# A hybrid decoder layer on one core: the third stage's loads on ScalarE, a chunk's queries in token halves, the second block's scores inside its product, the norm row a step earlier, accumulator banks kept

## The chip, the cores and the metric

One core of a Trainium2 chip runs the whole kernel. Its engines are TensorE (PE, with its weight loads shown as PEld), VectorE (DVE), ScalarE (ACT), GpSimd (POOL) and SyncE (SP), which only issues transfers. Transfers are issued by SP, ACT or POOL, in the order of the issuing engine's instructions, and run on 16 DMA engines that all share. The metric is the device time of one execution in microseconds (us); lower is better.

## What is computed

One layer of a hybrid decoder on a prompt of 4096 tokens and on 64 sample tokens (8 sequences of 8), all float32, model width 1024. Three groups of heads work on one projection:

```python
h = _rmsnorm(x, g_pre)
z = h @ w_in                                   # 1024 -> 2816
cb, cc, ch, cg, q, k, v, ag, mq, mg = _split_cols(z)
out_a = jax.nn.silu(cg) * cb * conv            # conv of width 3 over cc * ch
o_b = _window_prompt(q, k, v, sink_g)          # window of 128, 8 query heads, 2 kv heads, sinks
out_b = jax.nn.silu(ag) * o_b
o_c = _mem_attend(mq.reshape(n, t, MEM_HEADS, HEAD_DIM), mem_k, mem_v)   # 256 memory tokens
out_c = jax.nn.silu(mg) * o_c
y = jnp.concatenate([out_a, out_b, out_c], axis=-1) @ w_out
return x + _rmsnorm(y, g_post), new_conv, new_k, new_v
```

The sample tokens attend to cached keys and values of their own. New keys, values and conv states are outputs too.

## The kernel before

Matrices are multiplied at close to float32 precision by splitting each operand into a rounded high part (a copy by ACT) and the rest (a subtraction by DVE), and adding up three products: high x high, high x low, low x high.

**The input projection** (L927 on) runs in three stages over the 22 column tiles of `w_in`. Each stage goes over 8 token blocks of 2 x 260, and each block takes 7 products instead of 8 by sums of operands (`PRODUCTS`, L40). A step is one such product: for every column tile of the stage's pairs 12 matmuls of 128x260 into an accumulator bank, which DVE (or ACT for the first product) adds into `z` (`evict`). A step `i` also splits the operand of step i + 1 (`h_split`: ACT's copy, L364, and DVE's subtraction, L365) and, in the third stage, loads the operand of step i + 3 (`h_load`, L525) into one of four buffers. A load has to wait until the split of the operand that had the buffer is done. In the first stage the order of all engines is written out; from the second stage on a planner orders the instructions by its own costs and by when operands should be ready, except where the code asks for program order. The accumulators are two double banks for even and two for odd steps (`accumulator`, L148). At the start of the third stage all of these are closed and other pools opened: two small banks `psm` for the attention's first groups and the memory's keys, and a double and a single bank for each of the two kinds of step.

The third stage has three column pairs, so a step is 36 matmuls. In its gaps run the memory's keys (`mem_product`), and, from `third_jobs` (L808) at steps counted by n = 7 (b - 1) + p, the scores, softmax, transposes, masks and values of the first attention groups: `EARLY` gives the n of every piece of groups 0, 1 and 2, `PIECES` the pieces. The last block of the stage splits the output weights (`wo_split`, `wo_load`) into slots of the pool `wa`, as the input weights leave them.

**Attention and output** run over 33 blocks: 31 of 128 tokens, the block of the sample tokens, and the last one of 128. `Block.run` (L1516) multiplies the block's mixed heads with `w_out` in two halves of 512 columns, k = 0 to 7, three matmuls each: 48 matmuls of 128x512. Between them it runs events at given (half, k), from `events_of` (L1598). The event `values_and_scores(i)` at the block's beginning (in block 0 at k = 3) takes the scores of group i + 3, in four banks for the window and two for the memory, and the values of group i + 1 in the double bank `pv`. The softmax of a group is done by DVE and ACT, its weights are transposed by DVE in 32x32 squares, and 16 transfers of 64 KB (L1234) put the squares in place: on POOL's queue for groups 0 to 2, on SP's after that. POOL masks them (`masks`, L1248), and the values are due at the start of a later block. Each half of a block's product is scaled by the norm row `gpost` into `yn` (DVE, L1544) and squared (ACT, L1545); only then is its bank free. Queries and keys come in chunks of 256 tokens, two groups each (`chunk_load`, L1336), on POOL's queue, the queries in two transfers, one for the high and one for the low parts. The norm row is loaded at L1591, behind the projection. DVE and PE keep program order through these blocks, ACT in block 0 and POOL in blocks 1 and 2.

The sample tokens' attention is spread over blocks 26 to 30 by a table (L1594): `sample_window` (L1409) loads its mask into `smraw` (L1423) in its first part, makes scores and softmax in its second, transposes in its third (`swt`) and multiplies in its fourth.

Names: `x_6T` is a third-stage operand of block 6, `hi_` and `lo_` its parts, `c` an accumulator, `s` a group's scores and weights, `w` the weights in place, `wd` a masked copy, `ws` and `xs` window and memory scores, `pv` the values, `y` an output product, `mh` and `ml` the parts of the mixed heads.

Of the kernel before, what the change touches and what calls it, by code (L numbers as in the profile page):

```python
# [8 lines left out]
F32 = mybir.dt.float32  # L9
# [6 lines left out]
P = 128  # L16
# [35 lines left out]
def hybrid_layer(ctx: ExitStack, tc: tile.TileContext, a: dict):  # L52
# [65 lines left out]
    def open_phase(ph):  # L118
# [16 lines left out]
        if ph != 1:  # L135

            psa.close()
            bank = lambda name, bufs: psa.enter_context(tc.tile_pool(name=name, bufs=bufs, space=bass.MemoryType.PSUM))
            if ph == 0:
                pa2 = bank("pa0", 2)  # L140
            else:

                third["ps"] = bank("psm", 2)
                pa1 = {(tag, w): bank(f"p{tag}{w}", 1) for tag, w in (("y", 2), ("x", 2), ("x", 1), ("y", 1))}

    tp = natp = pa2 = pa1 = None

    def accumulator(i, w, name):  # L148
# [371 lines left out]
    def h_load(i):  # L520
        if i < len(steps) and steps[i][0] == 2:
# [3 lines left out]
            DMA.dma_start(t, hd[b][o])  # L525
# [315 lines left out]
    EARLY = ((15, 16, 17, 18, 19, 22, 24), (22, 23, 24, 25, 26, 29, 31), (30, 31, 32, 33, 34, 37))  # L841
    PIECES = (*(lambda g, n=n: g.early_scores(n) for n in range(4)), lambda g: g.early_turn(), lambda g: g.masks(), lambda g: g.values())
# [72 lines left out]

    last = NBLK - 1
# [10 lines left out]
    def input_projection():  # L927
        for i, (ph, b, p) in enumerate(steps):
# [78 lines left out]
    def open_attention():  # L1007
# [6 lines left out]
        ps = {tag: ctx.enter_context(tc.tile_pool(name=f"ps{tag}", bufs=1, space=bass.MemoryType.PSUM)) for tag in ("pv", *range(6))}  # L1014
# [45 lines left out]
    class Chunk:  # L1060
# [20 lines left out]
        def load_queries(self):  # L1081

            self.q = self.pool(True).tile([P, 12, CT], F32R, tag="q", name=f"q{self.c}").rearrange("p (j a) n -> p j a n", a=2)
            for part in range(2):
                G.dma_start(self.q[:, :, part, :], qd[part, 1:7, :, self.ts].rearrange("j p n -> p j n"))
# [28 lines left out]
    class Group:  # L1114
# [28 lines left out]
        def scores(self):  # L1143
            self.open_scores()
            bands = [psum(n, f"ws{self.b}_{n}").rearrange("p (h k) -> p h k", h=2) for n in range(4)]
            cross = [psum(4 + hh, f"xs{self.b}_{hh}").rearrange("p (j k) -> p j k", j=2) for hh in range(2)]
# [3 lines left out]
            tail(1)  # L1150
            self.crosses(cross)
# [85 lines left out]

        def early_turn(self):
            self.turn_band()
            self.turn_cross()  # L1240
# [511 lines left out]
```

## Time and profile before

| | us |
|---|---|
| median of 3 runs | 1502.98 |
| range of the runs | 1501.84 to 1504.06 |
| the profiled execution | 1499.29 |
| its span, first to last instruction | 1497.6 |

Input projection: the third stage begins at about 668 us and ends at 950 us; attention and output take the rest. The page gives, for each engine, the time in which it was busy as a share of the span, the share of the span in forty slices, the DMA queues, and the chain of work that ended last. A wait line reads: the engine and what it was about to do, then what ended the wait. Line L66 is the helper that keeps program order; there the names of the tiles tell the operation. "issue" is a wait that nothing in the profile explains. Where a wait is put down to something that had long been done, it was for another thing, often a transfer.

### The profile page before, as it was taken

To read this page: it belongs to the slowest core of one execution; us is meant where nothing else is said; L and a number is where in the kernel's file an instruction comes from. 1 tells how busy PE (TensorE), PEld (TensorE's weight loads), DVE (VectorE), ACT (ScalarE), POOL (GpSimd) and SP (SyncE) were. 2 spreads that over 40 slices of the span, in tenths; PEclk is the share of its full clock that TensorE was granted. 3 is DMA by queue.
4 is the path that set the end of the run, shared out by engine and by line. 5 is a ranking of instruction groups with operands and counts; after the bars stand their busy time and mean duration, and the time that the engine had idled before them with its cause. 6 is when DMAs were issued, how large, how long until landed. Compare 5 with 4: busy or idle time off the path is not lost.

```text
span 1497.6 us, 30845 instructions
## 1 busy us (share of the span) xinstructions
PE 1467.0 (98%) x11459; PEld 1341.6 (90%) x11459; DVE 1207.6 (81%) x1890; ACT 757.6 (51%) x1869; POOL 448.4 (30%) x623
## 2 busy tenths in 40 slices
PE   9999999999999999999999998899999999999998
PEld 9999999999999999999999988777777787777766
DVE  6779888898988777797678776878898898989843
ACT  6776666465422222254535443556555666656632
POOL 0223232212300000000003322265566566556531
PEclk9999999999999999999999999999999999999999
DMA  9989999887864333478967978899989988898663
GB/s 264 188 239 224 291 287 275 245 270 257 230 207 166 116 123 111 136 266 278 301 217 219 287 234 298 268 223 248 221 237 233 245 222 224 211 252 218 189 193 100
DMA packets 211964, 337.27 MB, mean 225 GB/s; under 512 B 55269, under 2 KB 125797, under 8 KB 211781
## 3 DMA queue, kind: packets, MB, share of 16 engines
q1 hardware_dynamic: 166629, 253.99, 56.7%
q0 software_dynamic: 43888, 78.15, 21.3%
q10 hardware_dynamic: 1296, 3.15, 0.7%
q8 instruction: 91, 1.49, 0.4%
q14 instruction: 60, 0.49, 0.1%
HBM read 192.48 MB, written 110.15 MB: 202 GB/s over the span
## 4 chain that ended last, share of the span: by engine, by line
PE 78%; DMA 7%; DVE 6%; issue 4%; POOL 2%; SPq 2%; ACT 1%; ACTq 0%; DVEq 0%; POOLq 0%
PE c L374 48%; PE y L66 19%; PE pv L66 5%; PE ws L66 2%; DMA w<-s 1%; PE y L1537 1%; PE xs L66 1%; PE mem_acc L789 1%; DMA x_7T<-hd_T 1%; SPq L1234 1%; DMA gpost<-in_gpost 1%; DVE s L66 1%; DMA vd<-v 1%; DMA wr_2A<-in_w_in 0%; DMA smraw<-in_smask 0%
## 5 line engine op out<-in xcount | busy, mean ns | idle before, releaser
L66 PE MATMUL y<-wo,mh 128*128 128x512 f32 x992 | 318.7, 396 | 0.0
L381 DVE TENSOR_TENSOR z<-c,z 128x520 f32<-128x520 f32 (+1 forms) x308 | 194.4, 644 | 81.6 <-PE c L374 78.2
L66 PEld LDWEIGHTS y<-wo,mh 128*128 128x128 f32 x992 | 186.5, 188 | 52.7 <-DVE wnm L66 5.0
L66 PE MATMUL y<-wo,ml 128*128 128x512 f32 x496 | 193.6, 390 | 0.0
L1193 ACT ACTIVATE s<-s,wnm 128x128 f32<-128x128 f32 x248 | 96.0, 388 | 45.7 <-DVE wnm L66 39.8
L1217 POOL TENSOR_SCALAR s<-s,xrd 128x256 f32<-128x256 f32 x120 | 57.7, 494 | 183.3 <-DVE xrd L66 106.1
L66 PEld LDWEIGHTS y<-wo,ml 128*128 128x128 f32 x496 | 93.5, 188 | 18.2
L1178 ACT COPY s<-ws 128x256 f32<-128x256 f32 x124 | 39.9, 379 | 92.4 <-PE ws L66 72.8
L748 POOL MEMSET negs<- 128x1 f32 x1 | 0.1, 98 | 266.6 <-PE c L374 266.6
L1567 POOL TENSOR_TENSOR xr<-yn,xr 128x1024 f32<-128x1024 f32 x29 | 69.6, 2398 | 21.5 <-ACT yn L1566 21.2
L66 DVE STREAM_TRANSPOSE s<-s 128x1024 f32<-128x1024 f32 x58 | 70.9, 1236 | 5.1 <-POOL s L1217 2.7
L1248 POOL TENSOR_SCALAR_AFFINE_SELECT wd<-w 128x512 f32<-128x512 f32 (+1 forms) x60 | 55.6, 926 | 49.5 <-DMA w<-s 28.8
L66 DVE TENSOR_TENSOR yn<-y,gpost 128x512 f32<-128x512 f32 x62 | 42.3, 683 | 29.5 <-PE y L66 22.7
L1545 ACT ACTIVATE y<-y 128x512 f32<-128x512 f32 (+1 forms) x64 | 37.4, 584 | 51.2 <-DVE yn L66 44.3
L66 PEld LDWEIGHTS ws<-kst,q 64*128 64x128 f32 x696 | 44.3, 189 | 17.2 <-issue 14.2
L1209 ACT ACTIVATE s<-xs,xnm 128x256 f32<-128x256 f32 x124 | 56.3, 461 | 4.4 <-DVE xnm L1207 3.7
L66 PE MATMUL ws<-kst,q 64*128 64x256 f32 x696 | 50.6, 291 | 6.6 <-issue 4.3
L66 DVE COPY_PREDICATED s<-wmask,ws 128x256 f32<-128x256 uint8 x116 | 44.9, 440 | 10.2 <-ACT s L1178 7.7
L287 ACT ACTIVATE nat<-nat 104x1024 f32<-104x1024 f32 x40 | 42.3, 1057 | 19.6 <-DMA nat<-in_x_p 19.4
L383 ACT COPY z<-c 128x520 f32<-128x520 f32 (+1 forms) x44 | 24.4, 555 | 52.8 <-PE c L374 50.1
L1566 ACT ACTIVATE yn<-yn,yst 128x1024 f32<-128x1024 f32 x31 | 35.7, 1151 | 26.2 <-POOL yst L1558 26.2
L1248 POOL TENSOR_SCALAR_AFFINE_SELECT w<-w 128x512 f32<-128x512 f32 x60 | 46.2, 790 | 1.8
(1001 smaller groups left out, 5015.9 us busy)
## 6 DMA issues: line engine op xcount, KB each, us to landing
w<-s SPq DMA_DIRECT2D x464, 64.0 KB
q<-qd POOLq DMA_DIRECT2D x32, 768.0 KB, 8.6
xr<-in_x_p SPq DMA_DIRECT2D x32, 512.0 KB
nat<-in_x_p SPq DMA_DIRECT2D x39, 416.0 KB
o_yp<-xr SPq DMA_DIRECT2D x31, 512.0 KB
md<-th POOLq DMA_DIRECT2D x48, 260.0 KB, 7.1
qd<-zh SPq DMA_DIRECT2D x48, 260.0 KB
qd<-z SPq DMA_DIRECT2D x48, 260.0 KB
```

The costliest lines, as they stand in the source:

```text
L66: return (lambda *args, **kw: tc.keep_in_program_order(fn(*args, **kw))) if on else fn
L287: S.activation(t[:RG], t[:RG], AF.Square, accum_out=r[:RG, i : i + 1])
L374: TE.matmul(bank[:, :HW], l, r, start=first and i == 0, stop=last and i == 3 * KH - 1)
L381: add = lambda dst, other: V.tensor_tensor(dst, c, other, op=ALU.add)
L1178: S.copy(to, squares(s3[:, :, P : 2 * P]))
L1193: S.activation(sm[:, h], sm[:, h], AF.Exp, bias=nm[:, h : h + 1], scale=SCALE, accum_out=den[:, h : h + 1])
L1209: S.activation(p[:, i], s[:, i].rearrange("p (a k j) -> p a k j", a=2, k=4), AF.Exp, bias=nm[:, i : i + 1], scale=SCALE, accum_out=den[:, ...
L1217: G.tensor_scalar(p[:, i], p[:, i], rd[:, i : i + 1], 0.5, op0=ALU.mult, op1=ALU.mult)
L1248: G.affine_select(out, src, pattern=[[32 * sign, 2], [0, 8], [sign, 32]], compare_op=op, fill=0.0, base=base * sign, channel_multiplier=-s ...
L1545: square = lambda acc=acc, p=p, c0=c0, c1=c1, end=end: S.activation((psum(2, "sq") if end else acc)[:m, : c1 - c0], acc[:m], AF.Square, sc ...
L1566: tc.keep_in_program_order(S.mul(yn, yn, st[:, 3:4]))
L1567: total = G.tensor_tensor(self.xr, yn, self.xr, op=ALU.add)
```

## The change

- The accumulators of the first two stages become four pools of one double bank each, taken in turn. The third stage keeps two of them and closes the other two for its small banks.
- In the third stage all operand loads but the first three are issued by ACT.
- Groups 0 to 2: the transposes of the window's and of the memory's weights become two pieces, a step apart. Group 1's masks and values move from n = 29 and 31 to 28 and 29.
- The norm row is loaded in the last block of the third stage, at its product 5, into a slot of `wa`.
- The queries of chunk 2 (groups 4 and 5) come in four transfers, by halves of 128 tokens, and behind the keys.
- `values_and_scores(1)` moves from the start of block 1 to k = 3 of its first half. Block 1's first half is summed in bank 5, and group 4's memory scores use banks 4 and 0, taken after the window's scores.
- The sample's mask is loaded by ACT, in program order; the transposes of the sample's window move from (29, half 0, k 4) to (29, half 1, k 2).
- The banks of the attention are opened in another order, which matches the new places of the third stage's.

```diff
+        bank = lambda where, name, bufs=1: where.enter_context(tc.tile_pool(name=name, bufs=bufs, space=bass.MemoryType.PSUM))
+        if ph == 0:
+            pa2 = {(tag, 0): bank(psa, f"p{tag}2") for tag in "yx"} | {(tag, 1): bank(own_banks, f"p{tag}3") for tag in "yx"}
+        elif ph == 2:
+            own_banks.close()
+            third["ps"] = bank(psa, "psm", 2)
+            pa1 = {("y", 2): pa2["y", 0], ("x", 2): pa2["x", 0], ("x", 1): bank(psa, "px1"), ("y", 1): bank(psa, "py1")}
...
         if pa1 is None:
-            return pa2.tile([P, 2, 512], F32, tag=tag, name=name, bufs=2)
+            turns[tag] += 1
+            return pa2[tag, (turns[tag] - 1) % 2].tile([P, 2, 512], F32, tag="c", name=name)
...
-            DMA.dma_start(t, hd[b][o])
+            (S if b or p > 2 else DMA).dma_start(t, hd[b][o])
...
-    EARLY = ((15, 16, 17, 18, 19, 22, 24), (22, 23, 24, 25, 26, 29, 31), (30, 31, 32, 33, 34, 37))
-    PIECES = (*(lambda g, n=n: g.early_scores(n) for n in range(4)), lambda g: g.early_turn(), lambda g: g.masks(), lambda g: g.values())
+    EARLY = ((15, 16, 17, 18, 18, 19, 22, 24), (22, 23, 24, 25, 25, 26, 28, 29), (30, 31, 32, 33, 33, 34, 37))
+    PIECES = (*(lambda g, n=n: g.early_scores(n) for n in range(4)), lambda g: g.turn_band(), lambda g: g.turn_cross(), lambda g: g.masks(), lambda g: g.values())
...
+    def gpost_load():
+        gpost.append(wa.tile([P, 2, 512], F32, tag="w", name="gpost").rearrange("p a n -> p (a n)"))
+        DMA.dma_start(gpost[0], a["gpost"].partition_broadcast(P))
...
+            if (ph, b, p) == (2, last, 5):
+                jobs.append(gpost_load)
...
-            for part in range(2):
-                G.dma_start(self.q[:, :, part, :], qd[part, 1:7, :, self.ts].rearrange("j p n -> p j n"))
+            for half in range(2) if self.c == 2 else (None,):
+                cs = slice(0, CT) if half is None else slice(P * half, P * half + P)
+                for part in range(2):
+                    G.dma_start(self.q[:, :, part, cs], qd[part, 1:7, :, self.ts][:, :, cs].rearrange("j p n -> p j n"))
...
+            cross_bank = lambda hh: psum((4, 0)[hh] if self.b == 4 else 4 + hh, f"xs{self.b}_{hh}").rearrange("p (j k) -> p j k", j=2)
...
-            chunks[c].load_queries() if c == 2 else chunks[c].load_keys()
-            chunks[c].load_keys() if c == 2 else chunks[c].load_queries()
+            chunks[c].load_keys()
+            chunks[c].load_queries()
...
-        DMA.dma_start(raw, a["smask"])
+        tc.keep_in_program_order(S.dma_start(raw, a["smask"]))
...
+                elif b == 1 and p == 0:
+                    acc = psum(5, "y1_0")
...
-              (27, 0, 3): window, (28, 1, 3): window, (29, 0, 4): window, (30, 0, 3): window}
+              (27, 0, 3): window, (28, 1, 3): window, (29, 1, 2): window, (30, 0, 3): window}
...
-        at(0, 0 if i else 3, values_and_scores, i)
+        at(0, 0 if i > 1 else 3, values_and_scores, i)
```

More of the change, by code (lines that the diff above doesn't have):

```diff
@@ L134, in open_phase @@
             tp = own.enter_context(tc.tile_pool(name=f"t{ph}", bufs=(7, 9)[ph]))
[L135 to L144, printed above, removed]
+        bank = lambda where, name, bufs=1: where.enter_context(tc.tile_pool(name=name, bufs=bufs, space=bass.MemoryType.PSUM))
[5 more added lines that the diff above has]
+            pa1 = {("y", 2): pa2["y", 0], ("x", 2): pa2["x", 0], ("x", 1): bank(psa, "px1"), ("y", 1): bank(psa, "py1")}
+    own_banks = ExitStack()
     tp = natp = pa2 = pa1 = None
+    turns = {"x": 0, "y": 1}
     def accumulator(i, w, name):
@@ L1012, in open_attention @@
         pa.close()
-        ps = {tag: ctx.enter_context(tc.tile_pool(name=f"ps{tag}", bufs=1, space=bass.MemoryType.PSUM)) for tag in ("pv", *range(6))}
+        ps = {tag: ctx.enter_context(tc.tile_pool(name=f"ps{tag}", bufs=1, space=bass.MemoryType.PSUM)) for tag in (*range(4), "pv", 4, 5)}
         vp = ctx.enter_context(tc.tile_pool(name="vp", bufs=4, side="right"))
@@ L1150, in scores @@
             tail(1)
+            if self.b == 4:
+                cross = [cross_bank(hh) for hh in range(2)]
             self.crosses(cross)
@@ L1589, in hybrid_layer @@
     blocks[1].load()
-    gpost = wa.tile([P, 2, 512], F32, tag="w", name="gpost").rearrange("p a n -> p (a n)")
-    DMA.dma_start(gpost, a["gpost"].partition_broadcast(P))
     mem0, mem1, window = sample_mem(0), sample_mem(1), sample_window()
```

11 lines of the change are left out of this document (5 added, 6 removed).

## The prediction

> **What bounds the kernel.** I read the page first, then TensorE's waits, then the places of those waits in the timeline and in short windows.
>
> ```profile
> span 1497.6 us, 30845 instructions
> PE 1467.0 (98%) x11459; PEld 1341.6 (90%) x11459; DVE 1207.6 (81%) x1890; ACT 757.6 (51%) x1869; POOL 448.4 (30%) x623
> ```
>
> TensorE (PE) is busy for 98% of the span, and the change takes no matmul away. So it can only win the time in which PE waits, and the time in which PE runs slowly after a wait. PE's waits of a microsecond or so and more, the kernel's first instructions aside (to the right of the name: us in total, times, longest):
>
> ```profile
> PE ws L66 <- issue: 4.3, 1, 4.3
> PE swt L66 <- DVE ssm L66: 3.6, 1, 3.6
> PE c L374 <- ACT hi_6T L364: 3.1, 1, 3.1
> PE pv L66 <- DMA smraw<-in_smask: 2.0, 1, 2.0
> PE ws L66 <- ACT y L66: 2.0, 1, 2.0
> PE ws L1046 <- DVE place L1291: 1.4, 2, 1.0
> PE c L374 <- DVE z L381: 1.0, 1, 1.0
> PE c L374 <- DVE lo_6T L365: 0.9, 1, 0.9
> ```
>
> A wait costs more than its length. In the next rows (stretch, length, busy time and count of PE, PEld, DVE, ACT, POOL, then granted clock, DMA share, GB/s) the clock behind three of these waits is 0.50 to 0.66:
>
> ```profile
> 904.00:908.00 4.00, 3.59 (x18) 3.59 (x19) 1.60 (x2) 1.06 (x1) 0.00 (x0) 0.57 0.81 181
> 1440.00:1444.00 4.00, 2.92 (x11) 2.19 (x11) 2.94 (x10) 1.35 (x6) 0.56 (x1) 0.50 0.91 257
> 1444.00:1448.00 4.00, 4.00 (x24) 2.23 (x24) 1.13 (x5) 2.63 (x5) 2.37 (x1) 0.66 0.45 105
> ```
>
> Busy time times the missing clock is 3.59 x 0.43 = 1.5 us in the first row, and 2.92 x 0.50 + 4.00 x 0.34 = 2.8 us in the other two. [...]
>
> The sum is made against the profiled execution, 1499.29 us around its span of 1497.6. The median of the runs, 1502.98, lies 3.7 us higher; the difference found is taken off it unchanged.
>
> **Part 1, the banks kept.** At the start of the third stage PE waits 1.0 us for the last evictions (z L381), because the new pools lie over the accumulator used last. Now that step starts on the bank pair that was used a step before, which DVE has emptied. Gain 1.0, nothing added.
>
> **Part 2, the third stage's operands on ScalarE.** 53 of the 56 loads at L525 leave SyncE's queue for ACT's.
>
> ```profile
> 889.41 3.58 SPq L855 DMA_DIRECT2D vn<-vq  x4
> 896.31 1.36 SPq L525 DMA_DIRECT2D x_6T<-hd_T  x1
> ACT hi_6T L364 <- DMA x_6T<-hd_T: 9.5, 1, 9.5
> SPq L525 <- DVE lo_2T L365: 12.3, 4, 3.9
> SPq L525 <- DVE lo_1T L365: 11.0, 4, 3.7
> 1438.58 0.45 ACTq L1371 DMA_DIRECT2D place<-in_cmv  x1
> ```
>
> The load of x_6T was issued at 896.31, behind stores on SP (vn, and the parts of q) that wait for results of DVE; ACT sat 9.5 us for it and PE lost 3.1 + 0.9 + 1.5 of clock = 5.5 us. On ACT nothing of that stands ahead of it. Against this, an issue takes 0.45 us of ACT's queue, 53 of them 24 us, on an engine that is busy for 51%; and a load that finds its buffer still held (SP waited some 3 us each time for lo) now holds up ACT, with the splits (hi, L364), evictions and exponentials behind it. The splits wait for PE anyway, so most of this is covered. I take 1.0 us of loss; the bounds are 0 and the slower rival below. Net 4.5. [...]
>
> **Part 3, the early groups.** Transposes one step apart, and the second group's masks one step and its values two steps earlier. That frees the two small banks sooner, for which the next scores waited 1.4 us (place L1291). But the weights have to be there:
>
> ```profile
> 753.22 14.44 PE c L374 x120
> 843.62 4.01 POOL L1234 DMA_DIRECT2D w<-s  x8 [2.69 <-DVE s L1229]
> 859.15 1.40 POOL L1248 TENSOR_SCALAR_AFFINE_SELECT w<-w 128x512 f32<-128x512 f32 x2
> PE pv L1046 <- DVE s L1182: 0.2, 1, 0.2
> ```
>
> A product of this stage costs 0.12 us and a step 36 of them, 4.3 us; two steps are 8.7. In the profile the group's masks end at 860.55, 17 us after its first store, and that latency is not touched. If PE's order follows the text, PE waits up to 8.7 us. This stage is ordered by the planner, though, which puts a product where its operands should be ready, and no value product of the stage waited over 0.2 us. Bounds 0 and 8.7, taken 2.0, near the row. Net -0.6.
>
> **Part 4, the second block's start.** Rows of PE's timeline (start, us) around blocks 0 to 2, and of the chain of waits for blocks 3 and 4:
>
> ```profile
> 963.82 0.39 PE L66 MATMUL y<-wo,mh 128*128 128x512 f32 x1
> 972.07 1.64 PE L66 MATMUL ws<-kst,q 64*128 64x256 f32 x11 [1.96 <-ACT y L66]
> 977.75 0.50 PE L66 MATMUL y<-wo,mh 128*128 128x512 f32 x1
> 988.55 0.39 PE L66 MATMUL y<-wo,mh 128*128 128x512 f32 x1
> 993.69 0.50 PE L66 MATMUL y<-wo,mh 128*128 128x512 f32 x1
> 1013.39 11.15 PE y L66 x48
> 1029.36 11.13 PE y L66 x48
> ```
>
> From the end of one block's products to the first of the next it takes 993.69 - 988.94 = 4.75 us where nothing waits, but 977.75 - 964.21 = 13.54 behind block 0: 8.8 lost. From block 2 to block 3 it is 19.70 us against 15.97 for the next period: 3.7 lost.
>
> ```profile
> 953.07 0.86 POOL L1085 DMA_DIRECT2D q<-qd  x1
> 956.22 0.70 POOL L1079 DMA_DIRECT2D kst<-qd  x1
> q<-qd POOLq DMA_DIRECT2D x32, 768.0 KB, 8.6
> 964.63 0.46 ACT L66 ACTIVATE s<-xs,xnm 128x256 f32<-128x256 f32 x1
> 966.91 0.69 DVE L66 TENSOR_TENSOR yn<-y,gpost 128x512 f32<-128x512 f32 x1 [4.13 <-DMA gpost<-in_gpost]
> 989.48 11.38 SPq L1234 DMA_DIRECT2D w<-s  x13
> 1007.04 1.20 ACT L1178 COPY s<-ws 128x256 f32<-128x256 f32 x4 [3.44 <-DMA vh<-vn]
> DMA packets 211964, 337.27 MB, mean 225 GB/s; under 512 B 55269, under 2 KB 125797, under 8 KB 211781
> ```
>
> Two things were late: the keys, third on POOL's queue behind 1.5 MB of queries, and the norm row (gpost), for which DVE sat 4.13 us and, through the evictions and squares of block 0, the score banks. After the change the norm row is there a step earlier, the keys go first, only half the queries are needed, and nine products (9 x 0.232 = 2.1 us) run before the scores. Queries in half-length rows may take as long as whole ones (8.6 us each) or half of that. At the worst end the loads land when all of them had landed before, 964.21 + 4.3 = 968.5, for scores that are now due at 967.2: bounds 0 and 1.3 of wait, taken 0, since the load that came last now comes first. What is late next: block 1's first product now writes bank 5, which ACT's last cross exponential (964.63 + 0.46, 965.1) holds until 0.9 us after block 0's end; and the second cross bank is bank 0, which has to be copied and masked first, as bank 3 has to be squared: 1.1 us, from DVE's 0.69 us pieces (bounds 0 and 2). So 2.0 of the 8.8 come back.
>
> Block 3 waits for block 4's weights: SP issues them until 1000.86, ACT's next copies (1007.04) wait for the landing, and the squares and values queue behind. The second half of these scores moves from 972.07 to 964.2 + 0.9 + 2.1 + 0.8 (twelve of the score products, from eleven in 1.64 at about half the clock) = 968.0, 4.1 earlier; PE's call for the values moves 6.8 earlier. That alone would add 2.7 us of wait; the sample mask's load (smraw), which SP issued at this place and on which PE's 2.0 us are put down, gives part back (128 x 768 floats, 393 KB, 1.7 us at the mean rate below). I leave block 3's 3.7 as it is; bounds all of it gone and 1.5 more. Net of part 4: 6.8.
>
> **Part 5, the sample window.** PE stands 3.6 us for ssm, and 2.8 us of clock follow: 6.4. The transposes move from k = 4 of the first half to k = 2 of the second, 18 products or 4.2 us later, which covers the wait. Then the last group's masks come due:
>
> ```profile
> 1451.18 1.40 POOL L1248 TENSOR_SCALAR_AFFINE_SELECT w<-w 128x512 f32<-128x512 f32 x2
> 1455.62 1.09 PE L66 MATMUL pv<-w,mv 128*64 128x128 f32 x16
> ```
>
> They end at 1452.6; PE asked for them 0.9 us after 1455.62, and now would at 1450.2. So 2.4 come back. The mask's own load on ACT runs two blocks early and costs one issue of 0.45. Net 4.0.
>
> **Sum.** 1.0 + 4.5 - 0.6 + 6.8 + 4.0 = 15.7 us, 1499.29 to 1483.6, and from the median 1502.98 to 1487.3. Differences under 0.2% (3 us) can't be told from none here.
>
> **Rivals.**
> - Everything is paid and nothing returned: 1.0 + 5.5 + 1.4 + 12.5 + 6.4 = 26.8, 1476.2. For it: most returned terms are latencies that a free queue may shorten. Against it: the two ends that I computed as late next.
> - The early values wait in full, 8.7 in place of 2.0: 9.0 gained, 1494. For it the 17 us from store to mask, against it the 0.2 us row.
> [...]
> - Slower: the loads hold up ACT. Each of the 53 waits there for lo as SP did, some 3 us, and the next split comes late. From 15.7 / 53 = 0.30 us of PE per load the change is a loss; at 0.5 us, a sixth of such a wait, it costs 26.5, of which 1.0 is in the sum, and ends at 1487.3 + 25.5 = 1512.8. [...] Against it: ACT's spare half, and the split's own wait for PE.
>
> **Chances.** Forecast 0.42; all paid 0.13; early values 0.15; loads as late 0.10; slower 0.20. Faster by over 0.2%: the first four, 0.80, less 0.02 for a mixture of returns that eats the sum, 0.78; within 0.2% 0.04, of that and of the slower rival's 0.20 near its point of no change; slower 0.18. The range goes from the all-paid case, 1476, to just above the early-values case and up to no change, 1502; the slower rival is left out.
>
> **What would show it.** Right: no wait at hi_6T and x loads on ACT's queue ahead of their splits; from block 0's last product to block 1's last some 18 us (24.7 before); clock 1.00 behind 968; no swt wait; a last wait at pv near the end. Wrong: new PE waits for hi or lo at every step of the third stage with ACT idle before a load; a wait at pv L1046 of some 8 us; a larger loss between blocks 2 and 3.

## The result, and the profile after

The changed kernel took 1507.56 us (median of 7 runs, 1506.35 to 1512.79) against 1502.98 before (now also of 7 runs, 1501.84 to 1506.36): a ratio of 1.0031 with a 95% interval of 1.0016 to 1.0047. It is slower by 4.6 us where 15.7 us of gain were forecast. Its profiled execution took 1508.84 us, 9.5 more than the 1499.29 of before: that one lay 3.7 under its median, this one lies 1.3 above.

The table cuts the spans at TensorE's instructions: the third stage runs from its first product to the first output product of block 0, and a block begins with its first output product. The column "again" is a second execution of the kernel before, "best" is the fastest kernel of this study, described with its experiment.

| us | before | again | after | best |
|---|---|---|---|---|
| up to the third stage | 668.2 | 671.9 | 668.3 | 668.8 |
| third stage | 281.9 | 284.6 | 293.7 | 279.1 |
| blocks 0 and 1 | 43.6 | 44.0 | 36.8 | 37.8 |
| blocks 2 to 4 | 51.7 | 51.6 | 56.9 | 52.3 |
| blocks 5 to 28 | 389.0 | 388.9 | 391.5 | 389.4 |
| block 29 to the end | 63.2 | 63.2 | 59.8 | 59.8 |
| span | 1497.6 | 1504.3 | 1507.0 | 1487.2 |

So the loss is in the third stage, +11.8, which the forecast had 3.9 shorter (4.5 less 0.6). Blocks 0 and 1 gain 6.8 as forecast, blocks 2 to 4 give 5.2 of it back, the tail gains 3.4, and 2.5 are lost in small waits in between.

The third stage of the kernel before, in the view of busy time by windows (stretch, its length, busy time and count of PE, PEld, DVE, ACT, POOL, granted clock, DMA share, GB/s):

```profile
668.20:950.10 281.90, 274.30 (x2243) 264.62 (x2244) 211.63 (x334) 129.70 (x255) 56.93 (x98) 0.99 0.81 256
```

The same view after; the second pair of rows is a wait inside the stage with what follows, the third pair the place of the sample window:

```profile
668.30:962.00 293.70, 279.32 (x2244) 268.31 (x2243) 213.64 (x339) 132.15 (x257) 60.42 (x100) 0.98 0.78 248
828.00:832.00 4.00, 1.80 (x12) 1.68 (x12) 3.44 (x6) 0.88 (x1) 2.16 (x4) 0.71 1.01 350
832.00:836.00 4.00, 4.00 (x26) 3.58 (x27) 2.33 (x5) 1.97 (x10) 0.75 (x1) 0.50 1.07 263
1440.00:1444.00 4.00, 4.00 (x24) 3.12 (x23) 0.55 (x3) 1.06 (x3) 2.19 (x4) 1.00 0.99 331
1444.00:1448.00 4.00, 4.00 (x39) 2.58 (x38) 0.00 (x0) 0.00 (x0) 0.55 (x1) 1.00 0.95 315
```

PE does the same work; it is idle for 14.4 us in place of 7.6 and busy 5.0 longer: 6.8 + 5.0 is the 11.8. The lower clock behind the waits, 0.98 over the stage in place of 0.99, accounts for some 3 of the 5.0 by an estimate from these rows (279.32 x 0.01). Here a wait of 3.6 us, up to 830.2, was followed by 0.71 and 0.50. In the last two rows the clock is 1.00 where it was 0.50 and 0.66 before: that wait is gone.

PE's waits after, the whole span, first instructions aside (us in total, times, longest):

```profile
PE pv L66 <- ACT y L1557: 6.3, 4, 3.9
PE pv L66 <- DMA vh<-vn: 4.1, 2, 2.5
PE ws L1054 <- DVE s L1196: 3.6, 1, 3.6
PE c L374 <- DVE lo_6B L365: 3.3, 2, 3.1
PE c L374 <- DVE lo_5T L365: 2.3, 1, 2.3
PE c L374 <- DVE lo_0T L365: 1.7, 1, 1.7
PE y L66 <- ACT y L1557: 1.7, 1, 1.7
```

The waits at hi_6T, z, gpost's evictions and swt have left the list. In their place stand waits of the third stage for splits (lo) and masked scores (s L1196), spread over its steps, and two groups in the output blocks.

What these splits and scores waited for is to be looked for on the queues. SP's longest waits for transfers between 668 and 962, after (the instruction that could not be issued, and the transfer whose end released it):

```profile
SPq L763 <- DMA x_1B<-hd_B: 4.6, 1, 4.6
SPq L180 <- DMA qd<-z: 3.8, 2, 3.4
SPq L1122 <- DMA vn<-vq: 3.4, 3, 2.5
SPq L180 <- DMA vn<-vq: 2.7, 1, 2.7
SPq L755 <- DMA x_1B<-hd_B: 2.5, 1, 2.5
SPq L180 <- DMA x_5T<-hd_T: 2.2, 2, 1.9
SPq L855 <- DMA x_5B<-hd_B: 2.0, 1, 2.0
```

and the only such rows before:

```profile
SPq L525 <- DMA x_5B<-hd_B: 0.8, 1, 0.8
SPq L1093 <- DMA qd<-zh: 0.7, 1, 0.7
SPq L525 <- DMA x_1T<-hd_T: 0.4, 1, 0.4
```

The row of L1122 is plain: it loads the stored values (vn) and waits for their store. The others are strange pairs: a store of q (L180) or of values (L855) has no data in common with a load of x_5T. What joins them is the semaphore that a transfer raises as it lands. In the changed kernel's trace the 1113 transfers of SP and ACT raise eight semaphores (numbers 100 to 107), one round for both engines: 1046 of the 1112 steps from one transfer to the next, in order of time, go to the next number. POOL's 240 have eight of their own (111 to 118, 30 each). Of the 1105 transfers of SP and ACT that raise a number used before, 1065 went out only after sixteen updates of it by the transfer that had used it last, whichever engine had issued that; 83 of the 17808 updates are missing from the trace. The sums below count the waits for the semaphore that the waiting transfer itself will raise. Before, with nearly all transfers of these two on SP's queue, the round was hardly ever felt: 2.2 us of such waits in the third stage. After, they are 47.9 us, 29.8 on SP and 18.1 on ACT. One place, put together from the transfer records (start, engine, semaphore, transfer):

```
815.1  SP  100  vn<-vq
817.4  SP  101  vn<-vq
818.7  ACT 103  x_4T<-hd_T
819.5  SP  102  vn<-vq
820.5  SP  104  vl<-vd
822.7  SP  105  qd<-zh
823.7  SP  106  qd<-z
824.2  SP  107  qd<-zh
826.4  ACT 100  x_5B<-hd_B
```

The load of x_5B stood on ACT for 4.9 us until the vn of 815.1, an unrelated store, had raised semaphore 100: sixteen updates from 821.14 to 826.29, and the instruction ahead of the load that waits for 100 ended at 826.33. ACT's timeline there (start, us, what; in brackets the idle time before and what ended it):

```profile
820.36 1.06 ACT L364 CAST hi_4T<-x_4T 128x1040 fp32r<-128x1040 f32 x1 [3.00 <-PE c L374]
826.37 0.33 ACTq L525 DMA_DIRECT2D x_5B<-hd_B  x1
827.27 0.65 ACT L1192 COPY s<-ws 128x256 f32<-128x256 f32 x2 [5.85 <-DMA w<-s]
827.80 1.07 ACT L364 CAST hi_4T<-x_4T 128x1040 fp32r<-128x1040 f32 x1
```

The chain of waits of the same place begins with the values' load:

```profile
820.54 7.53 DMA vl<-vd
```

and DVE's and PE's timeline goes on:

```profile
828.17 0.71 DVE L851 STREAM_TRANSPOSE vq<-vl 128x512 f32<-128x512 f32 x1 [4.20 <-DMA vl<-vd]
828.81 0.99 DVE L381 TENSOR_TENSOR z<-c,z 128x520 f32<-128x520 f32 x2
829.73 0.75 DVE L1196 COPY_PREDICATED s<-wmask,ws 128x256 f32<-128x256 uint8 x2
830.38 1.22 DVE L365 TENSOR_TENSOR lo_4T<-x_4T,hi_4T 128x1040 fp32r<-128x1040 f32 x1
830.20 1.12 PE L1054 MATMUL ws<-kst,q 64*128 64x256 f32 x5 [3.60 <-DVE s L1196]
```

ACT does nothing between 821.4 and 826.4 with score copies queued behind the load. The hold alone did not make these copies late: by the bracket at 827.27 they also waited for transposed weights (w<-s), which landed at 827.2, half a microsecond after the load had gone out. DVE stands for values (vl) that took 7.5 us to land; PE waits 3.6 us for the masked scores of both, and 4 us more, 832 to 836, pass at a granted clock of 0.50. A second change goes with it, in the view of DMA issues (last number: median us from issue to landing), after:

```profile
w<-s POOLq DMA_DIRECT2D x48, 64.0 KB, 6.6
```

It was 4.4 before, for the same 48 stores on POOL, which the change does not touch.

### The profile page after: what moved, and what is told of

The parts are those of the page before. It is cut to its first block, busy times and chain, and to the rows that moved or that the text cites. A ratio compares the mean times of both kernels' runs of the same rounds, so it can differ in the third digit from the quotient of the medians.

```text
span 1507.0 us, 30861 instructions
## 1 busy us (share of the span) xinstructions
PE 1469.9 (98%) x11459; PEld 1342.8 (89%) x11459; DVE 1207.8 (80%) x1890; ACT 757.5 (50%) x1869; POOL 454.3 (30%) x625
## 2 busy tenths in 40 slices
DMA packets 213532, 337.27 MB, mean 224 GB/s; under 512 B 55301, under 2 KB 127365, under 8 KB 213349
## 4 chain that ended last, share of the span: by engine, by line
PE 72%; DMA 9%; DVE 9%; issue 4%; ACT 2%; SPq 2%; POOL 1%; ACTq 0%; DVEq 0%; POOLq 0%
PE c L374 42%; PE y L66 18%; PE pv L66 5%; DMA w<-s 2%; PE ws L66 2%; DVE z L381 1%; PE y L1549 1%; PE xs L66 1%; DMA vh<-vn 1%; DMA vl<-vd 1%; DMA wr_2A<-in_w_in 1%; SPq L1248 1%; PE mem_acc L789 1%; SPq L855 1%; DMA vd<-v 1%
## 5 line engine op out<-in xcount | busy, mean ns | idle before, releaser
L66 PEld LDWEIGHTS y<-wo,ml 128*128 128x128 f32 x496 | 93.2, 188 | 18.1
L1579 POOL TENSOR_TENSOR xr<-yn,xr 128x1024 f32<-128x1024 f32 x29 | 69.7, 2402 | 21.4 <-ACT yn L1578 21.2
L1557 ACT ACTIVATE y<-y 128x512 f32<-128x512 f32 (+1 forms) x64 | 37.4, 585 | 52.6 <-DVE yn L66 45.7
L1207 ACT ACTIVATION_READ_ACCUMULATOR s<-s,wnm 128x1 f32 x248 | 46.3, 187 | 0.0
```

Of the source, the lines that this page charges most:

```text
L66: return (lambda *args, **kw: tc.keep_in_program_order(fn(*args, **kw))) if on else fn
L1207: S.activation(sm[:, h], sm[:, h], AF.Exp, bias=nm[:, h : h + 1], scale=SCALE, accum_out=den[:, h : h + 1])
L1557: square = lambda acc=acc, p=p, c0=c0, c1=c1, end=end: S.activation((psum(2, "sq") if end else acc)[:m, : c1 - c0], acc[:m], AF.Square, sc ...
L1579: total = G.tensor_tensor(self.xr, yn, self.xr, op=ALU.add)
```

## The experiments

**Which part of the change loses the time.** The loads or the early groups, or both: three kernels take parts of the change away, the fourth adds the loads alone to the kernel before.

```diff
-            (S if b or p > 2 else DMA).dma_start(t, hd[b][o])
+            DMA.dma_start(t, hd[b][o])
```

> The changed kernel with all operand loads of the third stage back on SyncE; the groups' new times and everything else stay. In the changed kernel the first output product starts at 962.09 us, in the kernel before at 950.05. Theory A (the loads on ScalarE cost it: ACT stands in front of loads, and the planner orders SyncE's other transfers anew): the third stage is back at its old length, first output product at about 950, time about 1507.6 - 12 = 1495.5. Theory B (the early groups' new times cost it): first output product stays at about 962, and the stall before x_6T returns on top, time 1507 to 1512.

For the groups, EARLY and PIECES are those of before:

```diff
-    EARLY = ((15, 16, 17, 18, 18, 19, 22, 24), (22, 23, 24, 25, 25, 26, 28, 29), (30, 31, 32, 33, 33, 34, 37))
+    EARLY = ((15, 16, 17, 18, 19, 22, 24), (22, 23, 24, 25, 26, 29, 31), (30, 31, 32, 33, 34, 37))
...
```

> The changed kernel with the early groups as before (both transposes in one step, group 1's masks and values at n = 29 and 31); the loads stay on ScalarE. Theory A (loads): first output product still at about 960, time 1505 to 1508. Theory B (groups): first output product at about 950, time about 1495.5. Theory C (neither alone, the two together press ACT and the transfers): both this and the run with the loads put back win a good part of the 12 us.

> The changed kernel with both the loads and the early groups as before; what is left of the change is the kept banks, the second block's start, the norm row and the sample window. By every theory the third stage has its old length (first output product about 949 to 950), and the attention behind it is as in the changed kernel, which gained 12.04 - 9.48 = 2.6 us there: time about 1507.6 - 12 = 1495.5. If the attention's later stalls (between the fourth and fifth block 5.5 us) hang on when the third stage leaves its transfers, it differs by some 5 us either way: 1490 to 1501.

The fourth is the kernel before with the new L525 alone.

> The kernel before with one edit: the third stage's operand loads on ScalarE (all but the first three). Theory A: it loses what the changed kernel lost in that stage, some 12 us and the 1 us that the banks gained there: first output product at 960 to 963, time 1513 to 1516. Theory B: it gains the 5.5 us of the stall before x_6T, first output product at 944.5, time 1497.5. Theory C: between them, within 4 us of 1503.

| kernel | ratio to before | third stage, us | waits for the round of semaphores, us | w<-s, us |
|---|---|---|---|---|
| loads back | 0.9983 (0.9967 to 0.9999) | 288.0 | 1.3 | |
| groups back | 1.0018 (0.9995 to 1.0041) | 292.6 | 31.5 | 6.0 |
| both back | 0.9977 (0.9957 to 0.9998) | 284.8 | 3.1 | 4.3 |
| loads alone | 1.0035 (1.0015 to 1.0055) | 290.9 | 35.0 | 6.1 |

The view of issues has no landing time for w<-s in loads back. The loads alone make the kernel before slower by 0.35%, 5.3 us. With and without them the third stage differs by 5.7 us (after, loads back), 7.8 (groups back, both back) and 6.3 to 9.0 (loads alone, the two executions of before). The groups move the stage by 1.1 with the loads on ACT and 3.2 without, and the times by less than their intervals. So it is the loads. In loads back the stall for which they were moved is there again, in PE's waits:

```profile
PE c L374 <- ACT hi_6T L364: 4.8, 1, 4.8
```

**How the loads cost it.** Candidates: ACT is held by a load that waits for its buffer (the slower rival of the prediction); the round of semaphores; values loaded late on SP (vl); chance. The first run is the kernel before once more, for the spread.

> The kernel before, unchanged, in a second profiled execution, as a measure of how far two executions of one program differ. In the first one the third stage (its first product to the first output product) took 281.85 us and the attention behind it 547.5. If the stage lengths repeat, both come out within 1 us, and what differs in the total comes from the first 110 us, where the five profiles so far lay up to 7.8 us apart in the same code. If they don't repeat, the stage differences of the changed kernels (3 to 12 us) mean little.

It took 1505.99 us in its one run. The blocks repeat within 0.4 us and the third stage came out 2.7 longer, so a single execution tells third stages apart by some 3 us, not less.

The next one keeps the loads' order and their bulk on SP and only lets ACT issue a sixteenth of each, which puts 53 more transfers in the round:

```diff
-            DMA.dma_start(t, hd[b][o])
+            if b or p > 2:
+                DMA.dma_start(t[8:], hd[b][o][8:])
+                S.dma_start(t[:8], hd[b][o][:8])
+            else:
+                DMA.dma_start(t, hd[b][o])
```

> The kernel before, with each of the 53 operand loads cut in two: SyncE moves 120 of the 128 partitions as before, ScalarE the other 8. So ScalarE issues as many loads and waits for the same buffers as with all loads moved, but its queue carries a sixteenth of the bytes, and SyncE's order of transfers stays. Theory A1 (ACT is held at the loads, and its splits and copies come late): third stage as long as with the loads moved (290.9 us against 281.85 before), time some 9 us up. Theory A2 (the loads in a queue of their own take DMA engines from the other queues: w<-s on POOL's queue took 6.0 to 6.6 us from issue to landing in the three runs with the loads moved, 4.3 and 4.4 in the two without): stage within 2 us of 281.85, w<-s at about 4.4. Theory A3 (SyncE's remaining transfers come in a worse order, vl behind vn): the stage as in A2, and VectorE's wait for vl at 3 to 5 us, not 13.5.

It took 1525.57 us (one run) with a third stage of 307.8, the longest of all. Its waits for the round were 73.0 us, with w<-s at 4.5 us as before. SP's waits for transfers there:

```profile
SPq L761 <- DMA x_2B<-hd_B: 6.8, 2, 4.3
SPq L526 <- DMA x_1B<-hd_B: 4.5, 2, 2.9
SPq L526 <- DMA qd<-z: 4.1, 4, 1.7
```

So the stage can get longer without the slow w<-s. That the waits for the round did it does not follow: besides issuing 53 transfers more, this kernel kept the 16 DMA engines busy for 0.89 of its 307.8 us, against 0.81 of 281.9 before, 274 us in place of 228 for nearly the same bytes.

The values' loads went to ACT as well, in the third run:

```diff
-        DMA.dma_start(t, vd[:, NS + 512 * k : NS + 512 * k + 512])
+        S.dma_start(t, vd[:, NS + 512 * k : NS + 512 * k + 512])
```

> The changed kernel with the eight loads of vl on ScalarE's queue as well, so that none of them stands behind the vn stores on SyncE. In the changed kernel VectorE waited 13.5 us for vl in the third stage, and two of PE's worst steps (6.4 us at 825 and 4.9 at 918) follow such a wait. Theory A3 (SyncE's order): those waits go, the stage comes from 293.75 us to 283 to 287. Theory A1 (ACT held): no gain or a loss, since ACT stands before eight more loads: 292 to 297. Theory A2 (shared engines): the same bytes in the same queues but one, 291 to 294.

1509.82 us (one run), third stage 299.4: no better. DVE waits for vl nearly as long as in the changed kernel, 12.5 us against 13.5; a place on ACT's queue does not bring the values sooner.

The fourth has the old groups, and ACT issues only the seven loads of block 6, where the stall was:

```diff
-            (S if b or p > 2 else DMA).dma_start(t, hd[b][o])
+            (S if b == 6 else DMA).dma_start(t, hd[b][o])
```

> The changed kernel with the early groups as before and only the seven loads of block 6 on ScalarE, all other operand loads on SyncE: the late load of x_6T is in that block. Against the run with both put back (third stage 284.8 us, ratio 0.9977) the wait for hi_6T and lo_6T, 1.8 + 1.0 us, goes. By A1 and A2 seven loads cost 7/53 of 6 to 9 us, about 1: stage 282 to 284, ratio about 0.997. If the cost sits in particular steps and not in each load, it is either nothing (stage 282) or one whole loss of 5 us (stage 287).

1497.27 us, ratio 0.9938 (0.9918 to 0.9958), third stage 282.6, 2.5 us of waits for the round. Beside groups back, which differs only in the 46 other loads, that is 10 us less in the stage and 0.8% of the time.

**Held engine or queue.** The next run lets ACT issue all 53, but each behind the split of two steps ahead, in a fixed order, so that its buffer is free when it is reached:

```diff
-            h_load(i + 3)
+            if ph < 2:
+                h_load(i + 3)
             if ph == 0 or b > 0 or p > 0:
                 h_split(i + 1)
+            if ph == 2:
+                h_load(i + 3)
...
```

with the load and the copy that makes hi kept in program order.

> The changed kernel with one thing different: on ScalarE each operand load stands behind the split of the operand two steps ahead of it, in program order. In the changed kernel the planner puts most loads directly behind the split whose rest, VectorE's lo, has to free the buffer, and ACT stood 43 us at 27 loads until that lo had ended. Here two later splits lie between. The bytes, the queues and the early groups are those of the changed kernel. Theory A1 (held ACT costs it): ACT's idle time ahead of loads falls below 15 us, the third stage from 293.75 to 283 to 288 us, ratio to the kernel before 0.995 to 1.000. Theory A2 (the loads' own queue takes DMA engines from w<-s and vl): ACT's idle time falls, the stage stays at 291 to 295, w<-s at 6 us or more.

1517.81 us, ratio 1.0076 (1.0055 to 1.0098). ACT's idle time ahead of the loads, summed over the stage, fell from some 55 us to 2.1 and the time did not come back. But the fixed order made a new wait in the stage's first steps:

```profile
PE c L376 <- ACT hi_0T L364: 6.9, 1, 6.9
```

Its price is known from the same order put on the kernel with only block 6 on ACT:

> The early groups as before and only block 6's seven loads on ScalarE (ratio 0.9938 as measured), now with those loads and all third-stage splits in program order, each load behind the split two steps ahead. ACT was held there 2.8 us once. If holding is what seven loads cost, up to 2 us more are won: ratio 0.9925 to 0.994. If the order of the splits binds the planner elsewhere, a loss of some us: 0.995 to 0.998.

1504.31 us, 0.9992 (0.9976 to 1.0008). Counted from the stage's fifth step to the first output product, clear of that wait, the stage takes 263.3 us with block 6 on ACT, 265.9 with the order fixed, 274.4 after, and 277.0 here: 277.0 - 2.6 is again the 274.4 of after, within the some 3 us of single executions. The medians agree: 0.84% lie between the two kernels with the order fixed, 0.80% between groups back and block 6 on ACT. An ACT that is hardly ever held by a load loses as much. That rival falls as a mechanism. Nor does the loss follow the sum of the waits for the round: 21.7 us of them here (19.6 on SP, 2.1 on ACT), 47.9 after.

On POOL's queue, whose transfers raise 111 to 118 in the trace above, the same 53 loads go as follows:

```diff
-            (S if b or p > 2 else DMA).dma_start(t, hd[b][o])
+            (G if b or p > 2 else DMA).dma_start(t, hd[b][o])
```

> The changed kernel with the 53 loads on POOL's queue, where w<-s of the early groups goes too. ScalarE has no load to wait at. Theory A1: no PE wait for hi or lo from a held ACT; but POOL takes its instructions in order and waits for VectorE's transposes (up to 20 us at a time before), so a load behind such a wait is late and PE waits for hi instead: stage between 284 us, if POOL is free, and over 300. Theory A2: w<-s at 6 us or more again and the stage at 291 or more. A short w<-s with a short stage speaks for A1, a long w<-s with a short stage against A2.

1494.55 us (one run), third stage 283.9, waits for the round 5.0. And, with the old banks and the old groups, then with the old banks and the new groups:

> The kernel before with the second block's start, the norm row and the sample window of the change, and the 53 operand loads on POOL's queue; banks and early groups as before. Transfers of POOL's queue have completion semaphores of their own, so SyncE has its eight for itself. Theory A4 (shared completion semaphores cost it): SyncE's waits for semaphores below 6 us as in the run with the loads on POOL (48 us together with ACT's in the changed kernel, 2.2 before), third stage 281 to 283.5 us, ratio 0.990 to 0.9925. Theory A2 (a further busy queue takes DMA engines from w<-s): POOL's w<-s is then behind the loads and the groups' weights come late: stage 286 or more, ratio 0.994 or more.

> As the first of these runs, with the early groups at the change's times. It prices that part where the loads don't disturb it. On SyncE's loads it cost 3.2 us of stage in one profiled pair and 0.9 us in the medians, on ScalarE's 1.1 us the other way round to nothing. Expected 0.5 to 3 us of loss: stage 0.5 to 3 us longer than in the first of these runs, ratio 0.0005 to 0.002 higher. If the earlier values are a gain once nothing else is late, the stage is up to 1.4 us shorter.

0.9942 (0.9924 to 0.9960) with a stage of 283.5, and 0.9924 (0.9900 to 0.9948) with 282.5. POOL is held by these loads too, for longer than ACT was: some 150 us of idle time ahead of them in the first of the two. The longest of its waits for them in that third stage are

```profile
POOL x_3B L526 <- DVE lo_2T L366: 9.9, 2, 5.3
POOL x_5T L526 <- DMA vn<-vq: 8.8, 1, 8.8
POOL x_6T L526 <- DVE lo_5T L366: 8.5, 1, 8.5
```

but what is queued behind them there is not missed. 53 equal transfers cost 10 us more of stage on ACT (293.7) than on POOL (283.9), though an issue took 0.33 us on ACT and some 0.55 on POOL in these two kernels. That more than issue time hangs on the queue is an estimate from these numbers; no run shows the issue time by itself.

**The banks.** Block 6 on ACT, with the accumulators' pools as before:

> The same kernel (early groups as before, only block 6's loads on ScalarE) with the accumulator banks and the attention's bank order of the kernel before. In all kernels with kept banks the third stage starts 1.1 to 1.2 us sooner and loses 1.24 to 1.27 us three steps later, at lo_0T (two of them more); without them neither shows. Expected: the z L381 wait of 1.0 us is back, the lo_0T wait of 1.7 is 0.5 or less, ratio within 0.1% of 0.9938. If the bank order of the attention matters too, the second block's start gets longer by 1 to 2 us and the ratio is 0.9945 to 0.9955.

1491.45 us, 0.9915 (0.9888 to 0.9943), third stage 282.8. The wait for z (1.0 us) is back at the stage's start and the one for lo_0T three steps later falls from 1.7 to 0.5. The ratio overlaps that of 0.9938 with the banks kept.

**Who makes the round slow.** Values' stores on POOL in the changed kernel:

```diff
-            DMA.dma_start(rows_of[:, :, ds], turned[ds].rearrange("p (b j) -> p b j", j=32))
+            G.dma_start(rows_of[:, :, ds], turned[ds].rearrange("p (b j) -> p b j", j=32))
```

> The changed kernel, operand loads on ScalarE, with the 32 vn stores on POOL's queue. Three queues stay busy and the bytes are the same, but SyncE and ScalarE together have 32 transfers fewer to pass through their eight semaphores, and vl no longer stands behind the stores. Theory A4: the waits for semaphores fall from 48 us to about 30, the stage from 293.75 us to 286 to 290. Theory A2: stage 291 to 295. POOL waits for VectorE's vq at each store; if that holds up w<-s and the masks, PE waits at pv or at the early scores, and the stage is longer than 295 with few waits for semaphores.

1520.14 us (one run). It decides nothing: POOL, busy with masks, was itself held, and the values and splits came late.

```profile
POOL vn L855 <- DVE vq L851: 36.5, 3, 32.4
```

**Blocks 2 to 4.** Here SP's list is long, after:

```profile
1028.51 0.53 SPq L1582 DMA_DIRECT2D o_yp<-xr  x1
1029.13 0.40 SPq L1103 DMA_DIRECT2D mix<-md  x1
1033.64 0.34 SPq L1504 DMA_DIRECT2D xr<-in_x_p  x1
1034.09 13.30 SPq L1248 DMA_DIRECT2D w<-s  x16
```

The load of the next rows (xr) waits 4.1 us, from 1029.5 to 1033.6, for the store of a block's output (o_yp) out of the same buffer to land, and the weights of a coming block (w<-s) queue behind it. ACT's and PE's rows at the other end:

```profile
1050.33 0.65 ACT L1192 COPY s<-ws 128x256 f32<-128x256 f32 x2 [7.79 <-DMA o_yp<-xr]
1051.63 1.97 PE L66 MATMUL pv<-w,mv 128*64 128x128 f32 x16 [3.95 <-ACT y L1557]
```

Two kernels try this. On the kernel with the loads on POOL and the rest of the stage as before, half of the weights' stores of groups 3 to 6 go to POOL:

```diff
-                    (DMA if b > 2 else G).dma_start(to[32 * k : 32 * k + 32, g], self.squares[32 * g : 32 * g + 32, k])
+                    (G if b < 3 or b < 7 and k % 2 else DMA).dma_start(to[32 * k : 32 * k + 32, g], self.squares[32 * g : 32 * g + 32, k])
```

> As the first of these runs, with half of the sixteen w<-s transfers of groups 3 to 6 on POOL's queue. Between the second and the fifth block the changed kernel returned 5.2 us of the 6.9 it had gained, the others 1 to 3.4; SyncE took 12 to 13 us there for sixteen transfers, 0.8 us each, against 0.63 later. If its window of eight sets that pace, two windows halve the time, the products of block 3 start 2 to 4 us sooner after block 2's, and the ratio falls by 0.15 to 0.25%. If POOL, which also masks and loads queries and keys there, becomes the late one, PE waits for the masks at pv and 1 to 3 us are lost.

1.0004 (0.9988 to 1.0019), and blocks 2 to 4 take 63.8 us: fewer stores on SP did not help here, and PE has a new wait:

```profile
PE ws L66 <- ACT y L1562: 6.6, 1, 6.6
```

The other leaves the output rows of the first four blocks unwritten, in the changed kernel:

```diff
-                    DMA.dma_start(dst, self.xr)
+                    if b > 3:
+                        DMA.dma_start(dst, self.xr)
```

> The changed kernel without the stores of its first four output blocks (0 to 3), whose rows of the output stay unwritten. In the changed kernel SyncE's load of xr stood 2.3 to 4.1 us for such a store to land, and w<-s stood behind it; from block 0's first product to block 5's it took 93.64 us, 95.33 before, where the forecast of 6.8 less would have been 88.5. If SyncE's order (store, xr, w<-s) is what gives the gain back, the stretch comes to 88 to 90 us. If it is the chain of softmax, squares and masks itself, or the bytes of queries, keys and mixed heads, it stays at 92 to 94. The third stage is the same program: 293.75 us again within 2 us if that length repeats.

1501.74 us (one run). Blocks 2 to 4 take 53.8 us against 56.9, and SP's timeline has no store to wait for:

```profile
1025.10 0.53 SPq L1103 DMA_DIRECT2D mix<-md  x1
1026.65 6.10 SPq L1248 DMA_DIRECT2D w<-s  x9
```

So 3.1 of the 5.2 us given back may hang on the order store, xr, weights on SP; the other 2.1 are not resolved. One execution does not settle it: the kernels with at most seven loads on ACT and no split stores took 52.3 to 55.4 us there with these stores in place. The third stage, untouched by the edit, came out at 292.6 (293.7 after).

**The best of it.** Banks and groups as before, the new start of the second block, the norm row, the sample window, and block 6's seven loads on POOL:

```diff
-            DMA.dma_start(t, hd[b][o])
+            (G if b == 6 else DMA).dma_start(t, hd[b][o])
```

> Banks and early groups as before, the second block's start, the norm row and the sample window of the change, and only block 6's seven loads on POOL's queue. The same with these loads on ScalarE gave 0.9915, all 53 on POOL's queue 0.9942. If block 6's loads are all that was late, and a queue with semaphores of its own costs nothing, the stage is 281 to 283 us and the ratio 0.990 to 0.992. If POOL's waits for the third group's transposes hold them, hi_6T waits 3 us or more and the ratio is 0.994 to 0.997.

1490.81 us against 1505.22 for before in the same set, 0.9916 (0.9898 to 0.9935): faster than both kernels, and not to be told from the 0.9915 with the same seven loads on ACT. PE's waits in its third stage, up to 950:

```profile
PE ws L1055 <- DVE place L1306: 1.8, 2, 1.5
PE c L375 <- DVE z L382: 1.0, 1, 1.0
PE c L375 <- DVE lo_6B L366: 0.9, 2, 0.7
```

No wait for hi_6T, none for scores or late splits of over 0.7 us, 2.0 us of waits for the round, and w<-s lands in 4.6 us.

## Why the prediction was wrong

**Part 2, loads on ScalarE: this step failed.** It said "I take 1.0 us of loss; the bounds are 0 and the slower rival below. Net 4.5." The gain had the right place: the stall at hi_6T goes, in the changed kernel and in the best one. Its size is not settled: the stage is 2.2 us shorter from both back to block 6 on ACT and 2.8 from before to the best kernel, while the medians of the first pair lie 0.39% apart, 5.9 us. The loss was not 1.0. Net, the loads cost 5.7 to 9.0 us in the third stage; with the 5.5 of the forecast gained back that is 11 to 14.5 us gross, 0.21 to 0.27 us for each of the 53. Seven of them on ACT, at the one place where a load was late, cost nothing that can be seen. The step counted ACT's issue time and the buffers that a load waits for, and did not ask what else a transfer waits for before it is issued.

**The slower rival had the direction and the engine, not the mechanism.** "The loads hold up ACT" gave 1512.8 at 0.5 us a load. With ACT never held the loss stayed. What goes with the loss in every kernel with the 53 loads on ACT is the round of eight semaphores that SP and ACT share (19.6 to 32.1 us of waits on SP and 2.1 to 21.2 on ACT, more with a sixteenth on ACT), and, but for that one, w<-s stores that land in 5.8 to 6.7 us in place of 4.4. The other kernels have less of both (1.2 to 7.5 us of waits in all; 4.3 to 5.2). No run shows that the round's waits suffice: with the sixteenth the DMA engines were busier as well, and with ACT's order fixed less than half of these waits went with the same loss. What is shown is the queue: the same loads cost nothing that can be seen on POOL's. How the net 5.7 to 9.0 divide between the round and the slower landing, and why w<-s lands later, stays open: no run here has the one without the other and the same transfers.

**Part 1, banks kept:** the 1.0 at the stage's start came, and 1.2 us or more were lost again three steps later at lo_0T, in every kernel with the banks kept. Nothing was forecast to return; the sum is nil.

**Part 3, early groups:** forecast -0.6; the runs put it at nothing that they can tell, with single executions on both sides (3.2 us longer without the loads, 1.0 shorter with loads on POOL). The full wait of 8.7 us did not come.

**Part 4, the second block's start:** blocks 0 and 1 gained 6.8, as forecast, and 5.6 to 7.1 in the other kernels with this part. That the 2.0 us of returns came out is partly luck: PE waited 0.3 us for bank 5 (at 976.05), where 0.9 was forecast, and the memory scores behind bank 0 took 0.4 longer, where 1.1 was; 1.25 more went into a wait for squares (y L1557) ahead of the values at 996.36, which the sum did not have. Then "I leave block 3's 3.7 as it is; bounds all of it gone and 1.5 more" was too narrow: 5.2 came back between blocks 2 and 4 in the changed kernel, 0.6 to 3.7 in the kernels with at most seven loads on ACT and no split stores. The prediction named the weights on SP as late, but took the time that SP needs to issue them for the cause; the store of the output rows ahead of xr was left out.

**Part 5, the sample window:** forecast 4.0, found 3.4 in the changed kernel and 3.0 to 3.6 in all others with it. The clock stays at 1.00 there. What it met instead is on PE's timeline at the end, 2.5 us in two waits and not the 2.4 us at the last masks, so that the near agreement is luck:

```profile
1455.98 0.50 PE L66 MATMUL y<-wo,mh 128*128 128x512 f32 x1 [1.68 <-ACT y L1557]
1460.76 0.41 PE L66 MATMUL smt<-ident,sq 128*128 128x128 f32 x2 [0.84 <-DVE sq L66]
```

Of the 25.1 us between the forecast and the profiled execution, the third stage has 15.7 (11.8 + 3.9), blocks 0 to 4 5.2, blocks 5 to 28 2.5, the start 1.1, the tail 0.6. The third stage alone would have used up the whole gain; the other 9.4 made it a loss. The two executions' places in their own runs, 3.7 and 1.3, are in this; the medians miss by 20.3.

## What to carry to other kernels

Here the loads moved to ACT's queue stayed in line with SP's transfers, since both raise the same eight semaphores: 47.9 us of waits for them in the third stage, 2.2 before. So list, for each transfer, what its issue waits for, semaphores too, before the move is costed at its issue time. It was enough to move the transfers that the profile showed late, 7 of 53; all 53 did well only on POOL (stages of 282.5 to 283.9 us, 293.7 on ACT), whose transfers raised other semaphores (5.0 us of waits for the round) and where little behind the loads was missed. Where a start is pulled forward, follow the same queue for some blocks: what was gained at the start, 6.8 us, was in good part given back, 5.2, here beside a load that waited 4.1 us for a store out of the same buffer.

## What was not expected of the hardware

Two executions of the same kernel, the one before, differ by 3.7 us up to the third stage and by 2.7 in it, while blocks and tail repeat within 0.4; in the kernels of this study the stage begins between 667.1 and 676.5 us, with the old banks and with the new. So single executions were compared by stage here. The landing of POOL's 64 KB stores went from 4.4 us to 6.6 when loads moved from SP to ACT, with the same 337.27 MB moved in all. And the clock did not go by the length of a wait alone: 2.0 us of PE's wait that ended at 1009.2 before were followed by a granted clock of 0.60 from 1009 to 1013, while 2.5 us that ended at 1015.2 after were followed by 1.00 from 1015 to 1019.
